# A hybrid decoder step on one core: the first head's projection made between the state space steps and read back from DRAM

## The chip, the cores and the metric

The kernel runs on one core of one Trainium2 chip. The metric is the device time of one execution in microseconds, the median of several executions. A core has TensorE (PE, with its weight loads as PEld), VectorE (DVE), ScalarE (ACT), GpSimd (POOL), SyncE (SP, which here issues most DMAs) and 16 DMA engines.

## What is computed

One layer of a hybrid decoder, for 1024 prompt tokens and 8 x 4 sample tokens (1056 rows), width 1024, in float32. One RMSNorm feeds one projection w_in, whose columns go to four attention heads (q, k, v, gate ga) and to a state space branch (u, gate gs). Both branches are gated, joined and go through w_out into the residual stream.

```python
xn = _rmsnorm(hp, norm_g[l])
q, k, v, ga, u, gs = _in_proj(xn, w_in[l], q_norm_g[l], k_norm_g[l])   # q, k normed per 64
o = _diff_attend(q, k, v, ...)           # softmax(q1 k1) - lam * softmax(q2 k2), times v
o_a = _attn_out(o, ga, subln_g[l], lam_init)              # norm, times silu(ga)
o_s, hr, hi = _s5_branch(u, gs, h0_re, h0_im, ...)        # scan; gelu; glu; times silu(gs)
hp = hp + jnp.concatenate([o_a, o_s], axis=-1) @ w_out[l]
```

Outputs are the new rows, the normed keys, the values and the last states, of prompt and samples.

## The kernel before, in words

A float32 product is made of three matmuls of rounded parts (high x high, high x low, low x high), all through the helper `mm` (L138). A weight block of 128 rows and 512 columns comes as a tile `wraw` (3 buffers) and is split into `ws` (9 buffers) by `split_w`: ScalarE rounds (L187), VectorE or GpSimd in turn subtracts (L190). The transposed input lies in SBUF as `xt` tiles, already split. PSUM has three buffers `acc` for projections, two each of `sc` and `tr`, one `pv`.

The program has three parts. **First phase** (`first_phase`, L330): the state space branch. The order of TensorE's work is written by hand in the table `UNITS` (L45); the other engines are ordered by the scheduler. A unit is a letter and a number: `C` a chunk of the u projection (24 matmuls 128x352, `u_part`), `G` a chunk of the gate projection (24 such matmuls, then two VectorE passes L411 and L413 around a ScalarE tanh L412, and a store on ScalarE's queue L414; 12 chunks in all, from the generator `gate`), `T` statistics of the rows, `D` their spread over columns (the `tr<-diag,ones` matmuls), `M` and `N` maps and kernels of a group of channels, `L`, `S`, `O` loading u, the states and the output of a group, `Z`, `H` reading z and the gates back, `Y` the glu (`acc<-z,ws`, 36 matmuls each), `A`, `B`, `Q`, `P`, `U`, `W`, `X` small ones. In the states VectorE and GpSimd run a long chain (`St`, `X`, `H`, L724 to L756) with TensorE before and after it.

**Heads** (`project`, L858, mixed by a model clock with `attention` and `sample_attend`, L232): for each of four heads and each pair j of token tiles, 2 x 24 matmuls with a 128-row tile of x as the stationary operand and 512 weight columns (q, k, v, ga of the head) moving. Then the aftercare: v is scaled into `vo`; `norm_qk` squares (ScalarE L846), reduces (VectorE L847), makes a reciprocal root by small operations (L850, L162 to L169) and multiplies (L854); `silu` (L902, L903) makes the gate. Some steps later `keep_qkv` (L905) transposes q and k (L913) and writes their rounded parts (L922 to L927) into a tile `pt`, 1536 wide, 6 buffers; the scores read it. The samples have 16 matmuls per head (`project_sample`, L932). After a head's last pair the weights of the next are loaded. Row tile t of the projection is in PSUM until its last reader is done.

**Output projection** (`finish`, `out_proj`, L1206 on).

```python
        w = self.load_w(self.w_in_head(0), KT)
        ...
        self.mix((self.project(w), 1.0), (self.attn, RATE1), (self.smp, RATE3), until=True)
```

## Time and profile before

| what | value |
|---|---|
| runs shown | 677.31 us median of 3 (675.5 to 678.51) |
| profiled execution | 677.01 us |
| its span, first to last instruction | 675.2 us |
| busy: TensorE matmuls, weight loads | 589.8 us (87%), 489.0 us (72%) |
| busy: VectorE, ScalarE, GpSimd | 488.6 us (72%), 296.5 us (44%), 160.2 us (24%) |
| mean granted TensorE clock | 0.959 |
| first 512-wide matmul of the heads | 231.2 us into the span |

The page of the profile gives busy time per engine, the span in 40 slices, the chain of waits that ended last and the costliest groups of instructions. The trace behind it answers closer: busy time by window, an engine's timeline with the idle time ahead of each piece and what ended it, groups of instructions with the mean duration of one, and DMA issues with the time to landing.

### The profile page before, as it was taken

Reading aid. Unit: us, or ns where it says so; the run is one execution under the profiler, and the core shown is the slowest. Engines: PE = TensorE matmul, PEld = TensorE weight load, DVE = VectorE, ACT = ScalarE, POOL = GpSimd, SP = SyncE. Lnnn points to the kernel's source line nnn. Section 1 sums busy time; section 2 is a strip of 40 time slices with the busy share of each in tenths; the row PEclk is TensorE's granted clock in tenths of the full one; section 3 lists DMA queues with packets and bytes.
Section 4 is the critical chain, followed back from the end, with each engine's and each line's share of the span. In section 5 each row is a group of like instructions: output and inputs, shape, how many; then the busy total and the mean of one; then the engine's idle time right before and its main releaser. Section 6 shows DMA issues by size and latency. Waiting matters only on the chain.

```text
span 675.2 us, 10961 instructions
## 1 busy us (share of the span) xinstructions
PE 589.8 (87%) x3490; PEld 489.0 (72%) x3490; DVE 488.6 (72%) x1536; ACT 296.5 (44%) x732; POOL 160.2 (24%) x165
## 2 busy tenths in 40 slices
PE   5928589559598999989999899998999988999997
PEld 4926488558487877768877678776787756886775
DVE  5978997999774446898668986689866898822111
ACT  6952232111363325565455654556545577411000
POOL 0682779677522400020000200002000020001100
PEclk9968789798988999999999999999999998999999
DMA  9755418242366440243012431124301257333221
GB/s 308 259 158 150 84 48 223 78 149 71 94 191 200 147 136 26 67 126 111 24 34 72 123 109 25 34 67 127 109 17 33 58 164 219 129 112 124 83 82 51
DMA packets 85735, 74.61 MB, mean 110 GB/s; under 512 B 8685, under 2 KB 74766, under 8 KB 85678
## 3 DMA queue, kind: packets, MB, share of 16 engines
q1 hardware_dynamic: 83374, 69.51, 34.3%
q10 hardware_dynamic: 2304, 4.41, 1.8%
q8 instruction: 28, 0.46, 0.3%
q14 instruction: 29, 0.24, 0.1%
HBM read 53.85 MB, written 20.04 MB: 109 GB/s over the span
## 4 chain that ended last, share of the span: by engine, by line
PE 43%; DVE 30%; DMA 9%; ACT 6%; POOL 6%; issue 5%; SPq 1%; POOLq 0%; DVEq 0%; ACTq 0%
PE acc L138 31%; PE sc L138 5%; PE pv L138 3%; DVE s L1036 3%; DMA xtok<-in_x 2%; PE tr L1061 2%; DVE ws L190 2%; DVE pt L927 2%; DVE pt L924 2%; DMA gz<-gsd 1%; POOL ws L190 1%; POOL gz L484 1%; DVE et L517 1%; DMA wraw<-in_w_out 1%; DVE s L164 1%
## 5 line engine op out<-in xcount | busy, mean ns | idle before, releaser
L138 PE MATMUL acc<-ws,xt 128*128 128x512 f32 x768 | 206.0, 405 | 0.4 <-DVE gz L508 0.4
L138 PEld LDWEIGHTS acc<-ws,xt 128*128 128x128 f32 x768 | 136.7, 189 | 26.4 <-issue 1.6
L190 POOL TENSOR_TENSOR ws<-wraw,ws 128x512 fp32r<-128x512 f32 x30 | 46.1, 1540 | 373.8 <-ACT ws L187 373.8
L138 PE MATMUL acc<-xt,ws 128*128 128x352 f32 x576 | 99.0, 332 | 8.4 <-ACT ws L187 7.8
L138 PEld LDWEIGHTS acc<-xt,ws 128*128 128x128 f32 x576 | 95.0, 193 | 11.2 <-ACT ws L187 8.1
L138 PE MATMUL acc<-ws,o 128*128 128x512 f32 x336 | 84.8, 400 | 4.5 <-ACT o L1222 1.8
L138 PEld LDWEIGHTS acc<-ws,o 128*128 128x128 f32 x336 | 62.9, 191 | 18.9 <-ACT o L1222 2.0
L1041 ACT ACTIVATE s<-s,mn 128x128 f32<-128x128 f32 (+7 forms) x64 | 49.4, 774 | 36.6 <-DVE mn L1036 36.2
L138 PE MATMUL sc<-pt 128*128 128x256 f32 (+1 forms) x320 | 57.6, 295 | 5.8 <-DVE pt L927 2.5
L138 PEld LDWEIGHTS sc<-pt 128*128 128x128 f32 x320 | 46.5, 189 | 22.2 <-DVE pt L927 5.9
L187 ACT ACTIVATE ws<-wraw 128x512 fp32r<-128x512 f32 x68 | 41.4, 626 | 38.2 <-PE acc L138 20.3
L1270 DVE TENSOR_TENSOR xres<-acc,xres 128x512 f32<-128x512 f32 x16 | 11.0, 690 | 51.9 <-PE acc L138 51.9
L138 PE MATMUL pv<-vo,wt 128*128 128x128 f32 x288 | 40.1, 279 | 0.0
L138 PEld LDWEIGHTS pv<-vo,wt 128*128 128x128 f32 x288 | 36.6, 191 | 3.5 <-ACT wt L1064 1.8
L190 DVE TENSOR_TENSOR ws<-wraw,ws 128x512 fp32r<-128x512 f32 x38 | 32.5, 858 | 7.0 <-ACT ws L187 7.0
L412 ACT ACTIVATE acc<-gs 128x352 f32<-128x352 f32 x12 | 5.6, 468 | 62.8 <-DVE gs L411 62.8
L138 PE MATMUL acc<-z,ws 128*128 128x352 f32 x144 | 25.8, 338 | 5.1 <-DVE gs L413 3.2
L138 PEld LDWEIGHTS acc<-z,ws 128*128 128x128 f32 x144 | 24.4, 198 | 6.4 <-DVE gs L413 3.5
L1061 PE MATMUL tr<-cn,s 128*128 128x128 f32 x144 | 26.0, 274 | 1.3 <-ACT wt L1064 0.8
L1036 DVE CUSTOM_DVE_ANT_0 s<-sc,cb 128x512 f32<-128x512 f32 (+3 forms) x48 | 26.3, 548 | 1.1 <-PE sc L138 0.7
L1046 DVE SCALAR_TENSOR_TENSOR s<-s,ls 128x128 f32<-128x128 f32 (+7 forms) x32 | 26.0, 812 | 0.4
L1064 ACT ACTIVATE wt<-tr 128x512 f32<-128x512 f32 (+3 forms) x48 | 22.9, 485 | 6.6 <-PE tr L1061 6.5
(289 smaller groups left out, 1028.9 us busy)
## 6 DMA issues: line engine op xcount, KB each, us to landing
wraw<-in_w_in SPq DMA_DIRECT2D x44, 256.0 KB, 3.1
xT<-in_xT SPq DMA_DIRECT2D x12, 352.0 KB, 7.2
xtok<-in_x SPq DMA_DIRECT2D x8, 512.0 KB, 5.1
cached<-in_cache_k SPq DMA_DIRECT2D x64, 64.0 KB, 1.9
cached<-in_cache_v SPq DMA_DIRECT2D x64, 64.0 KB, 1.9
...
```

The lines of the kernel that those rows point to most:

```text
L138: self.nc.tensor.matmul(out, lhsT, rhs, start=start, stop=stop)
L164: v.tensor_tensor(tmp, tmp, x, op=OP.mult)
L187: nc.scalar.activation(hi, raw, AF.Copy)
L190: (nc.vector if self.turn else nc.gpsimd).tensor_tensor(lo, raw, hi.bitcast(F32), op=OP.subtract)
L924: v.scalar_tensor_tensor(lo[ps], q[ps], self.gains[ps, 0:1], hi[ps].bitcast(F32), op0=OP.mult, op1=OP.subtract)
L927: v.scalar_tensor_tensor(kk[half[1]], k[ps], self.pkc("k_g")[ps], kk[half[0]].bitcast(F32), op0=OP.mult, op1=OP.subtract)
L1036: v.tensor_tensor_reduce(out=s[:, k0 + a0:k0 + a1], in0=q[:, a0:a1], in1=bias, op0=OP.add, op1=OP.min, scale=1.0, scalar=last, accum_out=m)
L1041: nc.scalar.activation(s[:, 0:L], s[:, 0:L], AF.Exp, bias=last, scale=-1.0, accum_out=ls[:, 2 * i + c:2 * i + c + 1])
L1046: v.scalar_tensor_tensor(wv, st[1][:, 0:L], cf, wv, op0=OP.mult, op1=OP.add)
L1061: nc.tensor.transpose(q[:, 128 * b:128 * b + 128], wv[:, 128 * (b0 + b):128 * (b0 + b) + 128], self.idn)
L1064: nc.scalar.activation(wt[:, 0:128 * bn], q[:, 0:128 * bn], AF.Copy)
L1270: v.tensor_tensor(x, a, x, op=OP.add)
```

## The change

Head 0's projection leaves the heads. Its eight weight blocks are loaded in two halves of 256 columns by a new unit `V` (`half_head`). A new unit `J` is one step of `first_head`: for one half and one of nine row tiles 24 matmuls 128x256 (16 for the sample tile, 64x256), a ScalarE copy into `ho` and a store on ScalarE's queue to `h_d` in DRAM; there are 18 of them, set between the other units. The table `UNITS` is written anew: the chunks C30 and C21 stand ahead of D0, and most gate chunks stand earlier. The projection then runs over heads 1 to 3. With each pair of head 1 comes a `stored_pair` of head 0: it reads 512 KB of `h_d` into `hx` (one buffer) and has the same aftercare as a projected pair. Queries and keys get tiles of their own, `qt` (1024 wide, 4 buffers) and `kt` (512 wide, 8 buffers); `vo` goes from 5 to 8 buffers, `ga` from 3 to 5; the program is built with a setting for a DMA scratch size.

```diff
-UNITS = ("M0 T0 C20 D0 U0 L0 W N0 M1 P0 C30 X U1 L1 C21 C32 S0 N1 C31 C22 U2 L2 O0 M2 G G U3 S1 G N2 L3 G O1 "
+UNITS = ("M0 T0 C20 C30 C21 D0 U0 L0 W N0 M1 P0 X U1 L1 C31 C22 C32 S0 N1 G U2 L2 G O0 M2 G G U3 S1 G G N2 L3 G V0 G G O1 M3 G P1 "
+         "G S2 J J N3 G V1 J J J S3 Q0 J J Z1 J A0 J J O2 Z0 J B0 Z2 J J O3 J H0 Z3 J J H1 J J H2 Y0 H3 Y1 Y2 Y3").split()
...
+VB = 8
+GB = 5
+HB = 1
...
-        w = self.load_w(self.w_in_head(0), KT)
+        w = self.load_w(self.w_in_head(1), KT)
...
+        hs, self.w0 = self.first_head(), []
...
+                elif c[0] == "V":
+                    self.turn = None
+                    self.w0.append([self.split_w(r) for r in self.half_head(int(c[1]))])
+                elif c[0] == "J":
+                    next(hs)
...
+    def half_head(self, half):
+
+        w = self.w_in_head(0)
+        for k2 in range(KT // 2):
+            raw = self.raws.tile([128, W], F32, name="wraw", tag="wraw", bufs=3)
+            r = raw.rearrange("p (k s c) -> p k s c", k=2, s=2)
+            for i in range(2):
+                self.nc.sync.dma_start(r[:, i], w(2 * k2 + i)[:, 2 * half:2 * half + 2])
+            yield raw
+
+    def first_head(self):
+
+        nc = self.nc
+        self.h_d = self.dr.tile([NTOK, W], F32, name="hd")
+        for half in range(2):
+            for t in range(9):
+                n = 128 if t < 8 else 32
+                a = self.acc()[:, 0:256]
+                for kt in range(KT):
+                    c = 256 * (kt % 2)
+                    wh, wl = (x[:, c:c + 256] for x in self.w0[half][kt // 2])
+                    if t < 8:
+                        xh, xl = (self.A[kt][:, z, 128 * t:128 * t + 128] for z in (0, 1))
+                        self.mm(a, xh, wh, kt == 0, False)
+                        self.mm(a, xh, wl, False, False)
+                        self.mm(a, xl, wh, False, kt == KT - 1)
...
+                o = self.ss.tile([128, 256], F32, name="ho", tag="ho", bufs=3)[0:n]
+                if t < 8:
+                    nc.scalar.activation(o, a, AF.Copy)
...
+                nc.scalar.dma_start(self.h_d[128 * t:128 * t + n, 256 * half:256 * half + 256], o)
+                yield
...
+    def stored_pair(self, j, st):
+
+        x = self.att.tile([128, 2, W], F32, name="hx", tag="hx", bufs=HB)
+        self.nc.sync.dma_start(x, self.h_d[256 * j:256 * j + 256, :].rearrange("(i p) c -> p i c", i=2))
+        vo = self.value(st, j)
+        for i in range(2):
+            self.nc.scalar.activation(vo[:, i, :], x[:, i, 256:384], AF.Copy, scale=self.xr[:, 2 * j + i:2 * j + i + 1])
+        self.pair(0, j, st, [x[:, 0], x[:, 1]])
...
-        for h in range(NH):
+        first = self.new_head()
+        for h in range(1, NH):
+            st = self.new_head()
             for j in range(4):
+                if h == 1:
+                    self.stored_pair(j, first)
+                    if j == 1:
+                        s = self.att.tile([32, W], F32, name="ssum", tag="ssum", bufs=1)
+                        nc.sync.dma_start(s, self.h_d[S:NTOK, :])
+                        self.sample_due(0, s, first)
...
-        pt = st["PT"][j] = self.pt("pt")
+        qt = st["Q"][j] = self.att.tile([128, 1024], F32R, name="qt", tag="qt", bufs=4)
+        kt = st["K"][j] = self.att.tile([128, 512], F32R, name="kt", tag="kt", bufs=8)
...
-    nc = bacc.Bacc("TRN2", target_bir_lowering=False, num_devices=1)
+    nc = bacc.Bacc("TRN2", target_bir_lowering=False, num_devices=1, dynamic_dma_scratch_size=1024)
```

Here `pair` holds what followed a pair's matmuls before (norm, gates, the due `keep_qkv`), and `value` hands out `vo`.

What this does to the order of the engines' work is shown at three places. The first is TensorE after the third group's states (`sc<-U,BT`, `tr<-U,BT`), ahead of the last group's map and kernel (`tr<-cn,W`, `tr<-G,bd`). Before:

```order
L138 MATMUL sc<-U,BT 64x145 x4
L138 MATMUL tr<-U,BT 64x145 x4
L138 MATMUL sc<-U,BT 64x145 x4
L138 MATMUL tr<-U,BT 64x145 x4
L690 MATMUL tr<-cn,W 128x128 x8
L138 MATMUL tr<-G,bd 32x128 x8
L138 MATMUL acc<-xt_84,ws 128x352 x3
```

Now the last rows of the second J (`acc<-ws,xt`, 256 wide) stand there:

```order
L141 MATMUL acc<-ws,xt_86 128x256 x3
L141 MATMUL acc<-ws,xt_87 128x256 x3
L141 MATMUL acc<-ws,xt_88 128x256 x3
L141 MATMUL acc<-ws,xt_89 128x256 x3
L141 MATMUL acc<-ws,xt_90 128x256 x3
L141 MATMUL acc<-ws,xt_91 128x256 x3
L737 MATMUL tr<-cn,W 128x128 x8
L141 MATMUL tr<-G,bd 32x128 x8
L141 MATMUL acc<-xt_84,ws 128x352 x3
```

Sixteen rows of three 256-wide matmuls, two J's, have come in between the states and the kernel.

The second place is TensorE in the first 512-wide matmuls of the heads, around the first transposes of a head's pair. Before, with 72 such matmuls ahead:

```order
L138 MATMUL acc<-ws,xt_89 128x512 x3
L138 MATMUL acc<-ws,xt_90 128x512 x3
L138 MATMUL acc<-ws,xt_91 128x512 x3
L913 MATMUL tr<-cn,qn 128x128 x4
L138 MATMUL acc<-ws,xt_84 128x512 x3
L138 MATMUL acc<-ws,xt_85 128x512 x3
L138 MATMUL acc<-ws,xt_86 128x512 x3
```

Now the transposes (L990) of head 0's first stored pair stand among the first 48 matmuls of head 1, and the first scores (`sc<-kt,qt`) too:

```order
L141 MATMUL acc<-ws,xt_85 128x512 x3
L141 MATMUL acc<-ws,xt_86 128x512 x3
L141 MATMUL acc<-ws,xt_87 128x512 x2
L990 MATMUL tr<-cn,qn 128x128
L141 MATMUL acc<-ws,xt_87 128x512
L990 MATMUL tr<-cn,qn 128x128 x3
L141 MATMUL acc<-ws,xt_88 128x512 x3
L141 MATMUL acc<-ws,xt_89 128x512 x3
L141 MATMUL acc<-ws,xt_90 128x512 x3
L141 MATMUL acc<-ws,xt_91 128x512 x2
L141 MATMUL sc<-kt,qt 128x128 x2
L141 MATMUL acc<-ws,xt_91 128x512
```

The transposes come after 35 wide matmuls of the heads, where they came after 72.

The third place is SP's queue at the same point (`gz<-gsd` reads gates, `osd<-gz` stores the branch, `TB` is the bias table). Before:

```order
L481 DMA gz<-gsd_1718 128x1056
L509 DMA osd<-gz 128x1056
L179 DMA wraw<-in_w_in 128x4x128
L977 DMA TB<-tbd 32x256 x2
L509 DMA osd<-gz 128x1056
L977 DMA TB<-tbd 32x256 x2
```

Now the first read of the stored head stands behind the weight load:

```order
L528 DMA gz<-gsd_1497 128x1056
L556 DMA osd<-gz 128x1056 x2
L182 DMA wraw<-in_w_in 128x4x128
L923 DMA hx<-hd 128x2x512
L556 DMA osd<-gz 128x1056
L1059 DMA TB<-tbd 32x256 x4
```

The stored pair's load is behind one weight load and ahead of the last store of the branch.

## Rows read from the trace of the kernel before

**Rows 1.** Part 1 of the page: busy us (share of the span) xinstructions.

```profile
PE 589.8 (87%) x3490; PEld 489.0 (72%) x3490; DVE 488.6 (72%) x1536; ACT 296.5 (44%) x732; POOL 160.2 (24%) x165
```

**Rows 2.** Part 4 of the page: the chain that ended last, by engine.

```profile
PE 43%; DVE 30%; DMA 9%; ACT 6%; POOL 6%; issue 5%; SPq 1%; POOLq 0%; DVEq 0%; ACTq 0%
```

**Rows 3.** Busy time by window: us, busy (x) of PE, PEld, DVE, ACT, POOL; PEclk, DMA share, GB/s.

```profile
38.00:134.00 96.00, 61.46 (x423) 56.31 (x424) 84.61 (x159) 27.42 (x60) 65.47 (x62) 0.82 0.43 116
134.00:155.00 21.00, 13.28 (x107) 11.68 (x105) 21.00 (x34) 5.75 (x13) 16.93 (x12) 0.86 0.45 136
155.00:231.00 76.00, 62.97 (x392) 59.29 (x392) 50.94 (x76) 28.87 (x51) 32.64 (x29) 0.93 0.45 142
231.00:305.50 74.50, 71.17 (x408) 55.00 (x409) 53.11 (x216) 36.12 (x99) 8.12 (x8) 1.00 0.33 94
305.50:560.70 255.20, 242.46 (x1484) 191.40 (x1483) 205.67 (x842) 143.92 (x388) 17.20 (x13) 1.00 0.26 76
560.70:676.00 115.30, 108.56 (x516) 86.61 (x514) 42.12 (x113) 23.96 (x56) 4.78 (x3) 0.99 0.33 109
```

**Rows 4.** TensorE's timeline, 38 to 231 us: start, us, work, [idle before <-releaser].

```profile
53.53 3.91 PE L138 MATMUL tr<-diag,ones 128*128 128x384 f32 x6 [15.78 <-DVE diag L314]
...
80.69 1.97 PE L690 MATMUL tr<-cn,W 128*128 128x128 f32 x8 [7.48 <-ACT St L724]
...
99.96 7.98 PE L138 MATMUL acc<-xt,ws 128*128 128x352 f32 x48
...
128.62 0.82 PE L138 MATMUL sc<-H,G 128*128 128x137 f32 x2 [7.31 <-DVE kk L700]
...
149.91 1.12 PE L690 MATMUL tr<-cn,W 128*128 128x128 f32 x4 [5.92 <-ACT St L724]
...
185.18 1.50 PE L138 MATMUL tr<-bias,rn 33*32 33x384 f32 x8 [7.13 <-ACT Z L775]
...
204.27 5.15 PE L138 MATMUL acc<-z,ws 128*128 128x352 f32 x22 [3.19 <-DVE gs L413]
```

**Rows 5.** TensorE's timeline after 231 us.

```profile
231.20 16.91 PE L138 MATMUL acc<-ws,xt 128*128 128x512 f32 x72 [0.39 <-DVE gz L508]
...
262.11 3.92 PE L138 MATMUL acc<-ws,xs 128*64 128x512 f32 x16
...
271.29 1.19 PE L138 MATMUL sc<-pt 128*128 128x256 f32 x8
272.32 1.32 PE L138 MATMUL acc<-ws,xt 128*128 128x512 f32 x5
```

**Rows 6.** Groups of VectorE, 231 to 600 us, forms apart: busy us, mean ns of one.

```profile
L190 DVE TENSOR_TENSOR ws<-wraw,ws 128x512 fp32r<-128x512 f32 x19 | 15.4, 810 | 3.0 <-ACT ws L187 3.0
...
L847 DVE TENSOR_REDUCE qss<-qn 128x4 f32<-128x256 f32 x32 | 13.1, 411 | 6.7 <-ACT qn L846 6.3
...
L163 DVE SCALAR_TENSOR_TENSOR qt<-qr 128x8 f32<-128x8 f32 x16 | 2.7, 168 | 0.5
...
L854 DVE TENSOR_TENSOR qn<-acc,qr 128x256 f32<-128x256 f32 x32 | 12.1, 418 | 0.6
...
L923 DVE CAST pt<-pt 64x256 fp32r<-64x256 f32 x32 | 9.2, 289 | 19.9 <-ACT pt L922 19.5
...
L924 DVE SCALAR_TENSOR_TENSOR pt<-tr,gains,pt 64x256 fp32r<-64x256 f32 x32 | 15.5, 483 | 0.8
```

**Rows 7.** ScalarE: a group of 231 to 600 us; a DMA issue in its timeline.

```profile
L846 ACT ACTIVATE qn<-acc 128x256 f32<-128x256 f32 x32 | 12.0, 374 | 0.0
...
183.57 0.33 ACTq L414 DMA_DIRECT2D gsd<-gs  x1
```

**Rows 8.** SP's timeline at 231 us; part 6 of the page: KB each, us to landing.

```profile
231.86 0.38 SPq L179 DMA_DIRECT2D wraw<-in_w_in  x1
...
xtok<-in_x SPq DMA_DIRECT2D x8, 512.0 KB, 5.1
```

**Rows 9.** VectorE's timeline: the last multiply of head 0's projection.

```profile
305.52 0.76 DVE L854 TENSOR_TENSOR qn<-acc,qr 128x256 f32<-128x256 f32 x2
```

More of the change, by code (lines that the diff above doesn't have):

```diff
@@ L416, in gate @@
                     self.gs_d[m] = d
-                yield
+                yield m
     def u_part(self, m, n):
@@ L856, in norm_qk, with new_head, pair, value @@
         return qn
+    def new_head(self):
+        st = {"ga": {}, "Q": {}, "K": {}, "V": {}, "kept": {}, "out": set()}
+        self.heads.append(st)
+        return st
+    def pair(self, h, j, st, accs):
+        qn = self.norm_qk(accs, 128, self.xe[:, 2 * j:2 * j + 2])
+        ga = st["ga"][j] = self.att.tile([128, 2, 128], F32, name="ga", tag="ga", bufs=GB)
+        for i in (0, 1):
+            self.silu(ga[:, i, :], accs[i][:, 384:512], self.xh[:, 2 * j + i:2 * j + i + 1])
+        vo = st["V"][j]
+        self.due.append((self.clock + DUE, lambda: self.keep_qkv(h, j, qn, vo, st)))
+    def value(self, st, j):
+        st["V"][j] = self.att.tile([128, 2, 128], F32, name="vo", tag="vo", bufs=VB)
+        return st["V"][j]
+    def stored_pair(self, j, st):
[5 more added lines that the diff above has]
+        self.pair(0, j, st, [x[:, 0], x[:, 1]])
+    def sample_due(self, h, s, st):
+        qn = self.sample_columns(h, s, st)
+        self.due.append((self.clock + DUE, lambda: self.keep_sample(h, qn, st)))
     def project(self, w):
@@ L919, in keep_qkv @@
             for c, ps in enumerate(half):
-                hi, lo, kk = (pt[:, 512 * z + 256 * c:512 * z + 256 * c + 256] for z in range(3))
+                hi, lo = (qt[:, 512 * z + 256 * c:512 * z + 256 * c + 256] for z in range(2))
+                kk = kt[:, 256 * c:256 * c + 256]
                 ot = half[1 - c]
@@ L1232, in out_proj @@
             yield None
-        PT, out = (self.heads[NH - 1][n] for n in ("PT", "out"))
+        Q, out = (self.heads[NH - 1][n] for n in ("Q", "out"))
         c0 = 0
```

42 lines of the change are left out of this document (20 added, 22 removed).

## The prediction

> **What bounds the kernel now.** I read the page's busy shares first. TensorE's matmuls are busy in 87% of the span, VectorE in 72% [rows 1], and the chain that ended last runs over TensorE for 43% and VectorE for 30% [rows 2]: neither alone sets the time. So the next view is busy time by stage [rows 3]. From 231 us to the end TensorE is the bound: 71.2 of 74.5 us, 242.5 of 255.2, 108.6 of 115.3. Before that it is not: in the three windows from 38 to 231 us it is busy for 61.5 + 13.3 + 63.0 = 137.7 of 193 us, 55.3 us idle, and VectorE for 156.6; from 134 to 155 us VectorE is busy all the time. TensorE's timeline [rows 4] names the idle stretches, in brackets with what ended each: 15.78 us before the spread step, then 7.48, 7.31, 5.92, 7.13 and 3.19 us, all ended by VectorE or ScalarE in the chain of the state space steps; these are 46.8, and pieces of under 3 us make up the other 8.5. So there is idle TensorE time in one stage and a full TensorE in the next.
>
> **What the change removes.** Head 0's projection goes out of the heads: 4 pairs of 48 matmuls 512 wide and 16 for the samples. A long run of them takes 16.91 / 72 = 0.235 us each, the 16 take 3.92 [rows 5]: 192 x 0.235 + 3.92 = 49.0 us, in a stage where TensorE has some 5% idle. If nothing else held it, the heads would be 49 us shorter.
>
> **What it adds between the state space steps.** The 18 steps J issue 16 x 24 = 384 matmuls 256 wide over all tiles and 2 x 16 narrow ones. A run of eight 256-wide ones starts at 271.29 and the next group at 272.32: 0.129 us each [rows 5]. The widths 352 (7.98 / 48 = 0.166) and 512 (0.235) extrapolate to 0.125, so I take 0.129: 416 x 0.129 = **53.7 us**. Bounds: half of a 512-wide one, 0.118, gives 49; the 0.166 of a 352-wide one gives 69, and I stay near the low end because the eight were measured at this width.
>
> **What of it lies in the gaps.** I go by the new order, gap by gap. The two u chunks moved ahead of the spread step (48 matmuls, 8.0 us) fill half of the 15.78. The gate chunks moved ahead of the second output step (4.0 us each) fill the 7.31 and 0.9 beside it. Two J's (3.1 each) ahead of the last kernel map fill 6.2 of the 5.92 and what is around it. The J's around the last two output steps and the glu steps fill 7.13, 3.19 and small ones, 12.2 in all. That is 34.6 us; the 7.48 stays. The stage grows by 53.7 - 34.6 = 19.1. A denser stage also wins back a little clock: the granted clock is 0.82, 0.86 and 0.93 in these windows [rows 3], and 22 matmuls after the 3.19 us wait took 5.15 us, 0.234 each where 0.166 is usual [rows 4]. I take 2 us, so **+17.1**. Bounds: 53.7 less 47 (all but the 7.48) is +7; with 20 filled it is +34, because every gate chunk needs two VectorE passes before its PSUM buffer is free (three buffers), and VectorE is full from 134 to 155.
>
> Small things of this stage. Eight weight splits of head 0 come earlier, four of them on VectorE at 0.81 us [rows 6]: 3.2 us against 36 us of VectorE idle in 38 to 231; without that cover, 3.2. Each J adds one ScalarE copy (a 128x256 one from PSUM takes 0.374 [rows 7]) and one issue on ScalarE's queue (0.33 in the timeline [rows 7]), 18 x 0.7 = 12.7 us, while ScalarE is busy for 62 of 193 us [rows 3]. The 16 half loads on SP's queue are 16 issues of 0.38 [rows 8]. I cost these at nothing. So with the wider rings, the two tiles for queries and keys (the same instructions), and the scratch setting: no rows change by it that I can see; if some buffer is short, that is inside the upper bound.
>
> **What the stored head costs in the heads.** The projection goes, its aftercare stays: per pair two reductions 0.411, nine small operations of about 0.166, two multiplies 0.418, four casts 0.289, two gate products about as long, four subtractions 0.48 [rows 6], 6.8 us of VectorE per pair, and about 2.9 for the samples: 4 x 6.8 + 2.9 = 30.1 us. Before, head 0's stretch, from 231 to the last multiply of its projection at 305.52 [rows 9], held one head's aftercare: 53.1 us of VectorE in 74.5 [rows 3]. Now the stretch of the first projected head (head 1) holds two, and more of head 0's attention: counting both orders row by row with these durations, VectorE gets 42 us more up to the last multiply of head 1, 30 of aftercare and 12 of attention. That is 53.1 + 42 = **95 us of VectorE**, against TensorE's 79 (the same 208 wide matmuls, 74.5, and 4 of scores). So this stretch changes its bound. It starts late too: the first stored pair needs 512 KB from DRAM, which SP issues behind the first weight load of the next head; that load is issued 0.7 us into the stage [rows 8], a 512 KB load lands 5.1 us after issue [rows 8], so about 6 us. Head 0's transposes stand behind 35 matmuls (8.2 us) in TensorE's order, with the pair's aftercare ahead of them, so TensorE waits there. Between the 1.00 that VectorE shows from 134 to 155 us and the 0.806 (205.7 / 255.2) of the steady heads, I take 0.97, nearer the first because little but VectorE would hold this stretch: 95 / 0.97 + 6 = 104 us, 25 more than TensorE's 79. The later stretches keep TensorE as bound. **Heads: -49 + 25 = -24.** Bounds: no late start and VectorE without any gap, 95 us, gives -49 + 16 = -33; occupancy 0.806 gives 95 / 0.806 + 6 = 124, so -49 + 45 = -4.
>
> The stored pairs share one buffer: the load of the second waits on SP's queue until VectorE is done with the first, and holds up what stands behind it there (weights of head 2, cache pages, stores of values). With some 25 us from pair to pair and a landing of 5.1, I cost that at nothing; were it not hidden, it is 5.1 us for each of three pairs, part of rival 2's price.
>
> **The sum.** 677.0 (profiled execution; 675.2 of span and 1.8 around it; the median of the runs shown is 677.3, 0.3 above) + 17.1 - 24 = 670.1, say **670 us**.
>
> **Weighed against a rule.** In the steady heads VectorE is busy for 205.7 and weight loads for 191.4 of 255.2 us, matmuls for 242.5 [rows 3]. The Trainium skill, "Perfetto Trace Analysis", section Identifying the Most-Contended Engine, says that matmul busy time is no good measure of TensorE and that one should set its weight-load share beside the occupancy of the other engines. By that, VectorE (81%) and not TensorE (75%) would be the engine to relieve, and matmuls taken away there would buy little: the second rival below, 690 us for 670. The trace speaks for TensorE in one respect: its idle time there is 12.7 us of 255.2, and the waits in it are short.
>
> **Rivals.**
> 1. *The gaps take nearly all of it and VectorE packs without gaps.* For it: 55.3 us idle against 53.7 of work. Against: the 7.48 and the first 15.78 lie where head 0's weights are not loaded yet. Growth 7 - 2 = 5, heads -33: 677 + 5 - 33 = 649.
> 2. *Slower: the first heads are paced by VectorE at its steady occupancy.* Place: the stretch of head 1. VectorE's operations there stand in chains with ScalarE (squares, tanh, copies) between them, so that it may not exceed the 0.806 seen. Price: 124 us for 79, gain 4 against a growth of 17.1: 677 + 17.1 - 4 = 690. It decides below an occupancy of 95 / 105 = 0.90, where the stretch takes 111 us and the gain equals the growth. For it: no stretch of the heads shows more than 0.81. Against: there TensorE was the bound.
> 3. *The gaps are not filled.* The gate chunks and J's wait for PSUM buffers that VectorE frees late, and shift the state space chain with them: 20 us filled, growth 34 - 2 = 32: 677 + 32 - 24 = 685.
> 4. *It does not do what it says.* The new order does show head 0's matmuls ahead of the last glu step and none behind it, so hardly: 677.
>
> **How the numbers follow.** My forecast (658 to 681 by itself) gets 0.46, rival 1 0.20, rival 2 0.17, rival 3 0.15, rival 4 0.02. A measurement of this kernel tells 0.5%, 3.4 us, from no change. Faster: 0.30 of the forecast and 0.20 of rival 1, 0.50. Within 0.5%: 0.11 + 0.03 + 0.03 + 0.02 = 0.19. Slower: 0.05 + 0.14 + 0.12 = 0.31. The range reaches from rival 1 to just beyond rival 2, 648 to 691; about one in ten lies beyond each end.
>
> **What would show it.** The first 512-wide matmul of the heads starts at about 231.2 + 17 = 248 us; later than 258 is rival 3, before 240 rival 1. In TensorE's timeline J's stand where the 5.92, 7.13 and 3.19 us waits were. From the first 512-wide matmul to the last multiply of head 1 it takes about 104 us, with VectorE over 95% busy and TensorE waiting for VectorE, the first wait being for the stored pair; 115 us or more with VectorE at 85% is rival 2. From there to the end the time is about the same as TensorE's work: no new waits. The prediction is wrong if the heads are shorter by under 10 us or over 40 us, or if the stage before them grows by more than 30.

## The result and the profile after

| | before | after |
|---|---|---|
| median of 7 runs each | 676.93 us (673.66 to 678.51) | 680.63 us (678.00 to 683.19) |
| ratio, 95% interval | | 1.0056 [1.0032, 1.0079] |
| profiled execution, its span | 677.01, 675.2 us | 678.00, 676.2 us |
| first 512-wide matmul of the heads | 231.20 us | 265.71 us |
| from there to the end of the span | 444.0 us | 410.5 us |

The change is slower by 0.56%; I had forecast 670 us. The profiled execution of after happens to be the lowest of its seven, so that the two spans differ by 1.0 us where the medians differ by 3.7. What happened is seen in either: the stage ahead of the heads grew by 34.5 us and the heads, up to the end, shrank by 33.5. The page, its parts 1 and 4, answers to [rows 1, 2]:

```profile
PE 596.3 (88%) x3698; PEld 502.8 (74%) x3698; DVE 467.8 (69%) x1537; ACT 304.8 (45%) x750; POOL 155.0 (23%) x165
PE 41%; DVE 29%; DMA 11%; POOL 6%; issue 6%; ACT 5%; POOLq 0%; SPq 0%; ACTq 0%; DVEq 0%
```

On the page nothing stands out: TensorE has 208 instructions and 6.5 us more (the narrower matmuls), VectorE 21 us less, and the chain still alternates between the two. The stages have to be looked at. Busy time by window of after, columns as in [rows 3]; the cuts are the third group's states (the first `sc<-U,BT` of that group), the heads' first 512-wide matmul, the last multiply of head 1's projection and the output projection:

```profile
38.00:161.69 123.69, 91.83 (x597) 85.91 (x595) 104.38 (x203) 35.27 (x73) 75.83 (x74) 0.86 0.44 123
161.69:265.71 104.02, 95.34 (x746) 92.42 (x745) 46.39 (x73) 40.60 (x77) 40.40 (x35) 0.97 0.46 136
265.71:374.60 108.89, 96.18 (x579) 70.24 (x580) 88.66 (x378) 62.56 (x167) 8.34 (x8) 0.97 0.42 121
374.60:557.20 182.60, 170.28 (x1068) 134.02 (x1067) 149.87 (x650) 108.63 (x300) 11.53 (x9) 0.99 0.25 73
557.20:676.20 119.00, 113.49 (x554) 91.78 (x553) 48.59 (x139) 28.01 (x67) 4.77 (x3) 0.99 0.32 105
```

The same view of before, cut at the same two places of the first stage, at 141.79 and 231.20 us:

```profile
38.00:141.79 103.79, 69.25 (x470) 63.89 (x471) 92.40 (x169) 28.23 (x62) 72.75 (x69) 0.84 0.46 125
141.79:231.20 89.41, 68.46 (x449) 63.39 (x448) 64.35 (x101) 34.02 (x62) 42.49 (x33) 0.90 0.42 131
```

Read these two against the first two of after. Up to the third states, TensorE's idle time was 103.8 - 69.3 = 34.5 us and is now 123.7 - 91.8 = 31.9: hardly anything was filled. The states came 19.9 us later, about as much as the five gate chunks take that were moved ahead of this point (24 x 0.166 = 4.0 us each). Behind it the idle time went from 21.0 to 8.7 us, so there the J's did fill 12.3, and the granted clock rose from 0.90 to 0.97. In all TensorE's idle time of the stage went from 55.5 to 40.5: 15.0 us filled.

TensorE's timeline of after, 38 to 280 us, answers to [rows 4]; the waits of 3 us and more, the third states, and the start of the heads:

```profile
54.56 2.90 PE L141 MATMUL tr<-diag,ones 128*128 128x384 f32 x4 [8.03 <-DVE diag L317]
...
83.53 1.11 PE L141 MATMUL tr<-G,bd 128*32 128x128 f32 x16 [6.08 <-POOL G L721]
...
102.83 0.83 PE L141 MATMUL sc<-H,G 128*128 128x137 f32 x2 [7.98 <-POOL H L798]
...
135.83 1.10 PE L141 MATMUL tr<-G,bd 128*32 128x128 f32 x16 [8.96 <-ACT BT L738]
...
161.69 0.71 PE L141 MATMUL sc<-U,BT 128*64 128x145 f32 x8
...
210.47 0.85 PE L141 MATMUL tr<-bias,rn 33*32 33x384 f32 x8 [3.01 <-ACT Z L822]
...
265.71 8.35 PE L141 MATMUL acc<-ws,xt 128*128 128x512 f32 x35
...
275.87 0.30 PE L990 MATMUL tr<-cn,qn 128*128 128x128 f32 x1 [1.82 <-DVE qn L898]
```

The first line is as planned: 15.78 before the spread step became 8.03. The 7.31 before the second output, the 5.92 before the last map and the 3.19 are gone, and the 7.13 is 3.01; in the glu steps waits of 2.47 and 2.13 us are left. But two waits stand here that [rows 4] does not have: 7.98 us at the first output (`sc<-H,G` at 102.83) and 8.96 us at the third group's kernel (`tr<-G,bd` at 135.83). In before, the same two places waited 2.71 and 1.39 us:

```profile
94.92 0.82 PE L138 MATMUL sc<-H,G 128*128 128x137 f32 x2 [2.71 <-POOL H L751]
...
116.37 0.67 PE L138 MATMUL tr<-G,bd 128*32 128x128 f32 x16 [1.39 <-POOL G L674]
```

So 7.98 - 2.71 + 8.96 - 1.39 = 12.8 us of what was filled ahead of the third states were given back.

**Where the 8.96 comes from.** The kernel's transposes need `BT`, which ScalarE copies out of PSUM. ScalarE's timeline of after, just ahead:

```profile
128.89 0.47 ACT L459 ACTIVATE acc<-gs 128x352 f32<-128x352 f32 x1 [10.02 <-DVE gs L458]
...
132.75 0.63 ACT L190 ACTIVATE ws<-wraw 128x512 fp32r<-128x512 f32 x1 [2.84 <-DVE gs L460]
134.70 0.47 ACT L459 ACTIVATE acc<-gs 128x352 f32<-128x352 f32 x1 [1.33 <-DVE gs L458]
135.10 1.07 ACT L738 ACTIVATE BT<-tr 128x512 f32<-128x512 f32 x2
```

The copy stands behind two tanh of gate chunks (L459) in ScalarE's order. The first of these waits 10.02 us for a gate's VectorE pass L458. Between the two, ScalarE issues that gate's store at 132.30, and this waits 2.84 us more for the gate's second pass, L460. VectorE makes both passes only after a group's scan. Its timeline, the end of that chain:

```profile
127.17 0.66 DVE L791 TENSOR_TENSOR X<-E_re,X 128x512 f32<-128x512 f32 x1
...
128.35 0.51 DVE L458 SCALAR_TENSOR_TENSOR gs<-acc,R 128x352 f32<-128x352 f32 x1
```

In before the copy stood ahead of such a tanh, so that only the tanh waited:

```profile
114.58 1.08 ACT L691 ACTIVATE BT<-tr 128x512 f32<-128x512 f32 x2 [0.53 <-PE tr L690]
...
124.70 0.47 ACT L412 ACTIVATE acc<-gs 128x352 f32<-128x352 f32 x1 [8.52 <-DVE gs L411]
```

**Where the 7.98 comes from.** The first output waits for the first group's scan chain on VectorE and GpSimd. That chain begins with a multiply into `X`. VectorE's timeline of before has it at 82.49 us:

```profile
82.49 0.68 DVE L730 TENSOR_TENSOR X<-E_re,St 128x512 f32<-128x512 f32 x1
```

That of after has it at 90.55, behind a weight split and a multiply of u:

```profile
80.94 3.09 DVE L193 TENSOR_TENSOR ws<-wraw,ws 128x512 fp32r<-128x512 f32 x1
...
88.49 2.13 DVE L490 TENSOR_TENSOR uT<-uT,R 128x1024 f32<-128x1024 f32 x1
90.55 0.67 DVE L777 TENSOR_TENSOR X<-E_re,St 128x512 f32<-128x512 f32 x1
```

Both stand there because TensorE now makes the u chunks earlier: the multiply is of a u chunk, and the split is of a gate's weights, whose buffer is free only when the u chunks are done with it. They make 5.2 of the 8.1 us; what made the rest was not followed up.

### The profile page after: what moved, and what is told of

It is laid out like the page before. It is cut to its first block, busy times and chain, and to the rows that moved or that the text cites. A ratio compares the mean times of both kernels' runs of the same rounds, so it can differ in the third digit from the quotient of the medians.

```text
span 676.2 us, 11416 instructions
## 1 busy us (share of the span) xinstructions
PE 596.3 (88%) x3698; PEld 502.8 (74%) x3698; DVE 467.8 (69%) x1537; ACT 304.8 (45%) x750; POOL 155.0 (23%) x165
## 4 chain that ended last, share of the span: by engine, by line
PE 41%; DVE 29%; DMA 11%; POOL 6%; issue 6%; ACT 5%; POOLq 0%; SPq 0%; ACTq 0%; DVEq 0%
PE acc L141 26%; PE sc L141 6%; PE pv L141 4%; DVE s L1117 3%; PE tr L1142 2%; DVE ws L193 2%; DMA ud<-uT 2%; DMA wraw<-in_w_in 1%; DMA hx<-hd 1%; PE tr L141 1%; POOL X L778 1%; DMA C<-in_c 1%; DVE qt L1002 1%; DMA osd<-gz 1%; DVE s L1127 1%
## 5 line engine op out<-in xcount | busy, mean ns | idle before, releaser
L141 PE MATMUL acc<-ws,xt 128*128 128x512 f32 (+1 forms) x960 | 209.8, 360 | 0.4 <-DVE gs L460 0.2
L141 PEld LDWEIGHTS acc<-ws,xt 128*128 128x128 f32 x960 | 149.2, 192 | 21.1 <-issue 3.3
L193 POOL TENSOR_TENSOR ws<-wraw,ws 128x512 fp32r<-128x512 f32 x30 | 40.4, 1352 | 344.9 <-ACT ws L190 267.7
L141 PE MATMUL acc<-xt,ws 128*128 128x352 f32 x576 | 101.1, 338 | 8.8 <-ACT ws L190 8.8
L141 PEld LDWEIGHTS acc<-xt,ws 128*128 128x128 f32 x576 | 98.0, 199 | 11.1 <-ACT ws L190 8.8
L141 PE MATMUL sc<-kt,qt 128*128 128x256 f32 (+1 forms) x320 | 57.7, 295 | 11.2 <-DVE mn L1117 4.3
L141 PEld LDWEIGHTS sc<-kt,qt 128*128 128x128 f32 x320 | 46.1, 190 | 25.9 <-DVE mn L1117 8.2
L1122 ACT ACTIVATE s<-s,mn 128x128 f32<-128x128 f32 (+7 forms) x64 | 49.5, 774 | 29.8 <-DVE mn L1117 23.5
L193 DVE TENSOR_TENSOR ws<-wraw,ws 128x512 fp32r<-128x512 f32 x38 | 30.4, 804 | 27.1 <-ACT ws L190 26.9
L1351 DVE TENSOR_TENSOR xres<-acc,xres 128x512 f32<-128x512 f32 x16 | 11.0, 689 | 53.2 <-PE acc L141 53.2
L1117 DVE CUSTOM_DVE_ANT_0 s<-sc,TB,mn 128x256 f32<-128x256 f32 (+1 forms) x56 | 24.7, 442 | 0.8
```

The lines of the kernel that those rows point to most:

```text
L141: self.nc.tensor.matmul(out, lhsT, rhs, start=start, stop=stop)
L193: (nc.vector if self.turn else nc.gpsimd).tensor_tensor(lo, raw, hi.bitcast(F32), op=OP.subtract)
L1117: v.tensor_tensor_reduce(out=s[:, k0 + a0:k0 + a1], in0=q[:, a0:a1], in1=bias, op0=OP.add, op1=OP.min, scale=1.0, scalar=last, accum_out=m)
L1122: nc.scalar.activation(s[:, 0:L], s[:, 0:L], AF.Exp, bias=last, scale=-1.0, accum_out=ls[:, 2 * i + c:2 * i + c + 1])
L1351: v.tensor_tensor(x, a, x, op=OP.add)
```

## The experiments

The theories. **A:** the places cost the time. TensorE's new order changed which instructions of ScalarE and VectorE stand ahead of the state space chain, and two moved places, the gate chunks ahead of the last two maps and the two u chunks ahead of the spread, make the chain late. **B:** 53 us of projection don't fit in this stage, wherever they are put. **C**, a form of B: any TensorE work put in the gaps delays the chain. A pair of numbers in what follows is the heads' first 512-wide matmul (before 231.20, after 265.71) and the ratio to before. The heads' start is that of one profiled execution each: two of the same kernel (e7 and e12) differ in it by 1.1 us, and e9, whose first stage is that of after, by 5.1 from after. So two or three microseconds of it are no evidence without a wait that explains them. Diffs of `UNITS` show the piece that differs.

**e1_map_before_chunks.** The change, with the third map ahead of two gate chunks.

```diff
...
-U3 S1 G G N2 L3 G V0
+U3 S1 N2 G G L3 G V0
...
```

> Theory A (queues): gate chunks and u chunks that were moved ahead put their VectorE passes, ScalarE tanhs and weight splits into queues in front of the state space chain, so idle TensorE time is moved and not filled. Rival theory B (TensorE): the stage grew because the steps J do not fit; moving the chunks cost nothing. Here the kernel map of the third group (N2) stands ahead of the two gate chunks instead of behind them. A: the 8.96 us wait for the copy of BT falls under 2 us, because that copy no longer stands behind two tanhs on ScalarE; the heads start at 257 to 259 us instead of 265.7, time 672 to 675 us. B: what follows is bound by the work of TensorE, the start stays at 264 to 267, time 679 to 682.

Measured: 677.90 us, 1.0016 [0.9992, 1.0039]; heads at 263.02, both between what A and what B expected. TensorE's timeline:

```profile
118.81 0.66 PE L738 MATMUL tr<-cn,W 128*128 128x128 f32 x4 [0.23 <-ACT St L772]
...
135.46 0.96 PE L142 MATMUL acc<-xt,ws 128*128 128x352 f32 x2 [3.62 <-DVE gs L461]
```

The 8.96 is gone, so its cause was the place. The heads start only 2.7 us earlier: the gate chunks, now behind the map, wait there for a gate's second VectorE pass (L461) that frees a PSUM buffer, the 3.62. A holds for the wait and was too large for the time.

**e4_u_chunks_back.** The change, with the u chunks where before has them, and with the first two gate chunks together ahead of the first output.

```diff
...
-C20 C30 C21 D0 U0 L0 W N0 M1 P0 X U1 L1 C31 C22 C32 S0 N1 G U2 L2 G O0
+C20 D0 U0 L0 W N0 M1 P0 C30 X U1 L1 C21 C32 S0 N1 C31 C22 U2 L2 G G O0
...
```

> The changed kernel with the u chunks where they were before (C30 and C21 not ahead of the spread step; gate chunks behind the first group's states). A: weight splits and u multiplications no longer stand ahead of the first group's states on VectorE, the chain starts at 83 to 85 us instead of 90.5, and the 7.98 us wait for H falls to 2 to 4: time 673 to 677. B: the gap of 15.8 us ahead of the spread step opens again and 8 us of TensorE work come back behind it: 681 to 689.

Measured: 678.33 us, 1.0019 [0.9988, 1.0049]; heads at 264.05.

```profile
54.48 4.08 PE L142 MATMUL tr<-diag,ones 128*128 128x384 f32 x6 [15.88 <-DVE diag L318]
80.62 1.97 PE L738 MATMUL tr<-cn,W 128*128 128x128 f32 x8 [6.27 <-ACT St L772]
...
132.53 1.11 PE L142 MATMUL tr<-G,bd 128*32 128x128 f32 x16 [9.90 <-ACT BT L739]
```

The 7.98 at the first output is gone and the 15.88 before the spread is back: filling the first gap had only moved it (8.03 + 6.08 + 7.98 = 22.1 us of waits up to the first output in after, 15.88 + 6.27 = 22.2 here). The wait falls as A expected, and further; the time lies above A's range and below B's. The intervals of e1 and e4 each overlap that of the change, so neither gain is shown by itself.

**e7_both_back and e12_both_back_again.** Both edits together, and the same kernel once more in five rounds.

> The edits of e1 and e4 together (third kernel map ahead of the gate chunks; u chunks where they were). A, if the two losses are separate: the heads start at 258 to 261 us, 673 to 676 us. If a wait that is taken away here turns up at the next buffer instead: start at 262 to 265, 677 to 680.

> The kernel of e7 once more, in more rounds, to tell it from the kernel before. If its gain over the changed kernel is real it stands at 672 to 676 us, 0.2 to 0.8% under the kernel before; if e7 was a lucky draw, at 677 to 680.

Measured: 674.54 us, 0.9985 [0.9939, 1.0032], heads at 260.58; and 675.93 us, 0.9993 [0.9975, 1.0011], heads at 261.68. The two places together are worth 4 to 5 us of the stage and turn the change from slower into no difference; the interval of the second, longer measurement lies wholly below the change's. The heads still start 30 us later than in before. So A's two places explain the change's loss, but not why the stage grows.

**e2_order_alone.** Before, with after's order of u and gate chunks and no projection in it (no V, no J).

```diff
...
-UNITS = ("M0 T0 C20 D0 U0 L0 W N0 M1 P0 C30 X U1 L1 C21 C32 S0 N1 C31 C22 U2 L2 O0 M2 G G U3 S1 G N2 L3 G O1 "
-         "M3 G P1 G S2 N3 Q0 G G S3 Z1 G A0 G O2 Z0 B0 Z2 O3 H0 Z3 H1 G H2 G Y0 H3 Y1 Y2 Y3").split()
+UNITS = ("M0 T0 C20 C30 C21 D0 U0 L0 W N0 M1 P0 X U1 L1 C31 C22 C32 S0 N1 G U2 L2 G O0 M2 G G U3 S1 G G N2 L3 G G G O1 "
+         "M3 G P1 G S2 N3 G S3 Q0 Z1 A0 O2 Z0 B0 Z2 O3 H0 Z3 H1 H2 Y0 H3 Y1 Y2 Y3").split()
...
```

> The kernel before with the new order of the u and gate chunks and without V and J: head 0 stays in the heads. A: the second output step starts near 150 us as in the changed kernel (129 before), and with five chunks fewer behind it the heads start at 236 to 243 us (231 before): 682 to 688 us. B: the order is neutral, heads start at 231, 675 to 679 us.

Measured: 689.07 us, 1.0178 [1.0130, 1.0225]; heads at 243.22, just beyond A's range, so 12.0 us are lost with the same work.

```profile
101.18 0.82 PE L138 MATMUL sc<-H,G 128*128 128x137 f32 x2 [8.08 <-POOL H L751]
...
134.17 1.11 PE L138 MATMUL tr<-G,bd 128*32 128x128 f32 x16 [9.16 <-ACT BT L691]
...
182.32 0.82 PE L138 MATMUL sc<-U,MT 128*128 128x137 f32 x2 [5.97 <-ACT St L724]
195.97 0.82 PE L138 MATMUL sc<-H,G 128*128 128x137 f32 x2 [6.62 <-POOL H L751]
220.29 0.66 PE L138 MATMUL acc<-z,ws 128*128 128x352 f32 x1 [8.41 <-ACT z L1290]
```

The two new waits come without the projection, so the order makes them. The last three are gaps that the gate chunks had covered; with the chunks gone forward they open, and in after the J's had to fill these first.

**e15_better_order_alone.** As e2, with the order of e7 instead.

```diff
...
-C20 C30 C21 D0 U0 L0 W N0 M1 P0 X U1 L1 C31 C22 C32 S0 N1 G U2 L2 G O0 M2 G G U3 S1 G G N2
+C20 D0 U0 L0 W N0 M1 P0 C30 X U1 L1 C21 C32 S0 N1 C31 C22 U2 L2 G G O0 M2 G G U3 S1 N2 G G
...
```

> The kernel before with the order of e7 and without V and J (as e2, with e7's order). e2 started its heads 12.0 us later than before. A sharper: the waits at the first output and the third map made most of that, so the start is at 233 to 238 us: 679 to 684. If five gate chunks ahead of the second output cost by themselves, it stays at 241 to 245: 687 to 691.

Measured: 685.48 us, 1.0121 [1.0095, 1.0146]; heads at 241.58, 10.4 us later than in before: the start is in the second branch's range, the time between the two. By the heads' start the two places are 1.6 of e2's 12.0 us, by the ratios some 4; the larger part comes with the moving of the five gate chunks itself (the one other unit that moves with them is Q0, the load of the glu's weights). TensorE's timeline:

```profile
154.66 0.71 PE L138 MATMUL sc<-U,BT 128*64 128x145 f32 x8
...
180.56 0.83 PE L138 MATMUL sc<-U,MT 128*128 128x137 f32 x2 [6.04 <-ACT St L724]
194.21 0.82 PE L138 MATMUL sc<-H,G 128*128 128x137 f32 x2 [6.70 <-POOL H L751]
218.80 0.66 PE L138 MATMUL acc<-z,ws 128*128 128x352 f32 x1 [7.40 <-ACT z L1290]
```

The third states come 12.9 us later than in before, for 19.9 in after: of the chunks' 20 us some 7 are now hidden. The gaps that the chunks had covered behind the states are open as in e2: from the states to the heads it takes 241.58 - 154.66 = 86.9 us, for 231.20 - 141.79 = 89.4 in before, though 20 us of chunks have left this part. So 17.5 of the 20 us had lain in gaps there. My sharper expectation of A fell here.

**e5_idle_matmuls.** Before, plus five units K of 24 matmuls 128x352 that nobody reads (5 x 4.0 = 20 us), about where after has its added gate chunks: gate chunks without VectorE or ScalarE work.

```diff
...
-S0 N1 C31 C22 U2 L2 O0 M2 G G U3 S1 G N2 L3 G O1
+S0 K N1 C31 C22 U2 L2 K O0 M2 G G U3 S1 G K N2 L3 G K K O1
...
+                elif c[0] == "K":
+                    a = self.acc()
+                    for kt in range(KT):
+                        for z in range(3):
+                            self.mm(a[:, 0:352], self.A[kt][:, 0, 128 * z:128 * z + 128], self.A[kt][:, 0, 0:352], kt == 0 and z == 0, kt == KT - 1 and z == 2)
...
```

> The kernel before, order and all, with five added chunks of 24 matmuls 128x352 whose results nobody reads (20 us of TensorE, nothing on any other engine): one ahead of the second kernel map, one ahead of the first output, one ahead of the third kernel map, two ahead of the second output, about where the change put its moved gate chunks. A: work of TensorE alone does fill the idle time there (7.48, 2.71, 1.39 and 7.31 us), so the heads start at 233 to 238 us (231.2 before): 679 to 684 us. Rival C (any work on TensorE in these places delays the chain, whatever its passes): start at 247 to 252, 693 to 698 us.

Measured: 684.20 us, 1.0104 [1.0077, 1.0131]; heads at 239.49, 8.3 us later, 1.5 us beyond A's range and far from C's. ScalarE's timeline has the `BT` copy behind a tanh, and the wait for that gate's second pass, here too, with no pass added anywhere:

```profile
126.92 0.47 ACT L417 ACTIVATE acc<-gs 128x352 f32<-128x352 f32 x1 [8.81 <-DVE gs L416]
...
130.69 1.09 ACT L696 ACTIVATE BT<-tr 128x512 f32<-128x512 f32 x2 [3.30 <-DVE gs L418]
```

So it is not VectorE's added work that did it. TensorE reaching the map one chunk later was enough for the scheduler to put the copy behind the tanh.

**e14_idle_matmuls_after_map.** As e5, with the third K behind the map.

```diff
...
-S1 G K N2 L3
+S1 G N2 K L3
...
```

> The kernel of e5 with the one idle chunk that stood ahead of the third kernel map behind it; the same 20 us of added TensorE work. In e5 that map's copy on ScalarE came to stand behind a tanh that waits for VectorE, and TensorE waited 9.7 us, as in the changed kernel, though no pass was added. If the place in ScalarE's queue and not the work is what costs (A in its sharper form), the wait goes, and the heads start at 230 to 234 us instead of 239.5: 676 to 680. If added TensorE work as such delays the chain (C), the start stays at 238 to 241: 682 to 686.

Measured: 679.45 us, 1.0049 [1.0027, 1.0071]; heads at 235.56, 4.4 us later than in before for the same 20 us, between the two branches and nearer to A's.

```profile
118.33 0.67 PE L138 MATMUL tr<-G,bd 128*32 128x128 f32 x16 [1.69 <-ACT BT L696]
```

One unit's place was worth 3.9 us of the stage, and 15.6 of 20 us of bare TensorE work are hidden. C falls as a general rule: this stage has room for matmuls. Up to the third states these 20 us cost 6.7 (148.47 for 141.79). The same 20 us as gate chunks, with their VectorE and ScalarE passes and at partly other places, cost 12.9 there in e15 and 19.9 in after.

**e3_third_of_j.** After, with only the first of the three products for the prompt rows in J; the two products with a low part are left out of head 0's projection.

```diff
...
-                        self.mm(a, xh, wh, kt == 0, False)
-                        self.mm(a, xh, wl, False, False)
-                        self.mm(a, xl, wh, False, kt == KT - 1)
+                        self.mm(a, xh, wh, kt == 0, kt == KT - 1)
...
```

> The steps J make one of their three products for the prompt rows (the two with low parts are left out): 256 of 384 matmuls, about 31 us of TensorE, go away; all else stays. A: the J's stand mostly in gaps and cost the stage about 13 us net, so 9 to 15 us are saved: 665 to 672. B: the J's are the growth of 34 us, so 25 to 33 us are saved: 648 to 656.

Measured: 665.23 us, 0.9814 [0.9765, 0.9863]; heads at 250.61. Taking away 256 matmuls (16 x 16, at the 0.128 us each that after shows for them, below: 33 us) brings the heads 15.1 us forward. So about half of what was taken away had lain in gaps, as A expected, and about half had been paid for. With two thirds of J gone the heads still start 19.4 us late, of which e2 gives 12.0 to the order alone.

**e8_steps_early.** After, with before's order of u and gate chunks, and the J's put in the early gaps instead, where the gate chunks were; it needs 12 buffers of split weights instead of 9, and `vo` and `ga` one less each.

```diff
...
-UNITS = ("M0 T0 C20 C30 C21 D0 U0 L0 W N0 M1 P0 X U1 L1 C31 C22 C32 S0 N1 G U2 L2 G O0 M2 G G U3 S1 G G N2 L3 G V0 G G O1 M3 G P1 "
-         "G S2 J J N3 G V1 J J J S3 Q0 J J Z1 J A0 J J O2 Z0 J B0 Z2 J J O3 J H0 Z3 J J H1 J J H2 Y0 H3 Y1 Y2 Y3").split()
+UNITS = ("M0 T0 C20 D0 U0 L0 W N0 M1 P0 C30 X U1 L1 C21 C32 S0 N1 C31 C22 V0 U2 L2 J O0 M2 G J G U3 S1 J G N2 L3 J G J "
+         "O1 M3 G J P1 G S2 V1 J J N3 J G G S3 Z1 G Q0 J A0 G J O2 Z0 J B0 Z2 J O3 H0 J Z3 G J H1 G H2 J J J Y0 H3 Y1 Y2 "
+         "Y3").split()
...
-VB = 8
-GB = 5
+VB = 7
+GB = 4
...
-        ws = (self.fp if more else self.wp).tile([128, 2, W], F32R, name="ws", tag="ws", bufs=NMORE if more else 9)
+        ws = (self.fp if more else self.wp).tile([128, 2, W], F32R, name="ws", tag="ws", bufs=NMORE if more else 12)
...
```

> The u and gate chunks in the order of before, and the steps J, which put no pass on VectorE, into the early gaps: one ahead of the first output, three ahead of the second, the rest as the change has them. For that three more ws buffers (12), with vo 7 and ga 4. A: the early idle time is filled by J's, the heads start at 250 to 257 us: 662 to 671. Rival C: the start stays at 264 or later, 677 to 684.

Measured: 699.56 us, 1.0336 [1.0306, 1.0366]; heads at 278.18. The time is in neither theory's range. TensorE's timeline:

```profile
103.62 2.71 PE L142 MATMUL acc<-ws,xt 128*128 128x256 f32 x11 [9.08 <-DVE ws L194]
```

The first J waits 9.08 us for a weight split that VectorE makes late, and holds up TensorE's order behind it. That is one cause of the 12.5 us more than in after; the others were not followed up.

**e10_one_u_chunk and e11_u_chunk_at_wait.** e7 with one u chunk ahead of the spread (e10), and also the next one ahead of the second map (e11).

```diff
...
-C20 D0 U0 L0 W N0 M1 P0 C30 X U1 L1 C21 C32 S0 N1 C31 C22
+C20 C30 D0 U0 L0 W N0 M1 P0 X U1 L1 C21 C32 S0 N1 C31 C22
...
```

And e11 against e10:

```diff
...
-C32 S0 N1 C31 C22 U2
+C32 S0 C31 N1 C22 U2
...
```

> The kernel of e7 with one u chunk (C30) ahead of the spread step and the other (C21) where it was. In e7 the copies of the first group's states on ScalarE stand behind the zero fill of C30's tile, which waits 10.3 us for GpSimd. A: with C30 earlier that wait goes, the 7.45 us wait ahead of the second kernel map falls under 3 us and the first output is no later than in e7 (about 96 us); the heads start at 255 to 259 us, 669 to 673. If the weight splits that C30 lets loose stand ahead of the state chain on VectorE, as in the changed kernel, the first output comes at 100 or later and the start stays at 260 to 263: 674 to 678.

> The kernel of e10 with the u chunk C31 ahead of the second kernel map instead of behind it; a u chunk has only a ScalarE copy behind it. A: it fills what is left of the wait there, start 1 to 3 us earlier than in e10: 667 to 672. If its copy on ScalarE stands ahead of the states' copies, the chain is later by as much and nothing is gained: as e10 or up to 3 us more.

Measured: 690.93 us, 1.0202 [1.0179, 1.0225], heads at 276.78; and 686.91 us, 1.0134 [1.0103, 1.0165], heads at 273.87. No branch expected that. TensorE's and VectorE's timelines of e10:

```profile
92.43 1.94 PE L738 MATMUL tr<-cn,W 128*128 128x128 f32 x8 [19.82 <-DVE W L563]
```

```profile
76.78 0.68 DVE L778 TENSOR_TENSOR X<-E_re,St 128x512 f32<-128x512 f32 x1
...
91.60 0.68 DVE L563 TENSOR_TENSOR W<-W,Wt 128x512 f32<-128x512 f32 x1
```

The first scan chain starts at 76.78, 5.7 us earlier than in before, and the product `W` that the second map needs now stands behind the whole chain on VectorE. TensorE waits 19.82 us. In e11 the same wait is 18.07. One chunk of 4 us, moved, costs 276.78 - 260.58 = 16.2 us of the stage.

**e9_casts_on_gpsimd and e13_two_hx** ask about the heads. e9 is after, with head 0's query casts on GpSimd instead of VectorE; e13 is e7 with two buffers for the stored pair, each pair loaded one ahead.

```diff
...
-                v.tensor_copy(hi[ot], hi[ps].bitcast(F32))
+                (g if h == 0 else v).tensor_copy(hi[ot], hi[ps].bitcast(F32))
...
-                v.tensor_copy(lo[ot], lo[ps].bitcast(F32))
+                (g if h == 0 else v).tensor_copy(lo[ot], lo[ps].bitcast(F32))
...
```

> The changed kernel with the 16 casts of head 0's queries on GpSimd instead of VectorE (16 x 0.289 = 4.6 us off VectorE in the first stretch of the heads). If VectorE paces that stretch by its amount of work, it gets 4 to 6 us shorter: 675 to 677. If it is paced by TensorE or by chains over several engines: no change, 679 to 682, or longer if GpSimd's casts are slower than VectorE's.

```diff
-HB = 1
+HB = 2
...
+        self.hx = []
+        self.load_stored(0)
...
-    def stored_pair(self, j, st):
-
+    def load_stored(self, j):
...
+        self.hx.append(x)
+
+    def stored_pair(self, j, st):
+
+        x = self.hx.pop(0)
+        if j < 3:
+            self.load_stored(j + 1)
...
```

> The kernel of e7 with two buffers for the stored pairs, each pair's load issued one pair ahead. If part of the first stretch of the heads (109 us, 12.7 us of it without TensorE) is waiting for these loads, the waits of head 0's transposes (6.1 us in the changed kernel) fall under 3 us and the time is 2 to 4 us under e7. If VectorE's chain of the aftercare is what they wait for, the load is already hidden and the time is that of e7 within 1 us.

Measured: e9 681.74 us, 1.0084 [1.0056, 1.0112]. Its window of the first stretch of the heads:

```profile
270.83:379.00 108.17, 95.72 (x576) 69.59 (x575) 85.09 (x355) 62.90 (x167) 15.34 (x24) 0.97 0.42 119
```

VectorE has 3.6 us less to do than in after, and the stretch is 0.7 shorter: the amount of VectorE's work doesn't pace it by itself. (A cast takes 0.41 us on GpSimd here and 0.30 on VectorE in after, so the chain through the casts did not get shorter; which of the two made the result is not told apart.) (The stage ahead, which the edit doesn't touch, took 5 us longer in this execution, the longest of e9's four; the heads to the end are 683.0 - 270.83 = 412.2 us, for 410.5.) e13: 675.07 us, 0.9975 [0.9954, 0.9996], the best version that does all the work: heads at 262.33, 408.6 us to the end for 410.4 in e7. The waits of head 0's transposes fall from 6.1 to 4.5 us, not under 3, and the time is 0.9 us under the same kernel with one buffer (e12), in the second branch's range. It is 0.25% faster than before, only just clear of no difference, and, by the two ratios, 0.8% faster than the change.

## Why the prediction was wrong

**The step that failed is "What of it lies in the gaps".** The sum was 53.7 of new work, less 34.6 in gaps, less 2 of clock. J's two groups among TensorE's instructions of after, 161.7 to 265.7 us, columns as in [rows 6]:

```profile
L141 PE MATMUL acc<-ws,xt 128*128 128x256 f32 x384 | 49.2, 289 | 0.3 <-DVE gs L460 0.2
...
L141 PE MATMUL acc<-ws,xs 128*64 128x256 f32 x32 | 4.0, 277 | 0.0
```

- *The added work:* 49.2 + 4.0 = 53.2 us, 0.128 each (the mean of one, 289 ns, counts the overlap of one with the next); forecast 53.7. TensorE's busy time from 38 us to the heads rose by 187.2 - 137.7 = 49.5, so the other matmuls took 3.7 us less, with the granted clock at 0.86 and 0.97 for 0.84 and 0.90; forecast 2.
- *The gaps:* 15.0 us were filled, not 34.6, and 49.5 - 15.0 = 34.5 is the growth; forecast 17.1, with a bound of 34. The moved chunks are the term that failed. Their 8.0 + 8.2 us were to lie in gaps, so the new order alone should have made the stage 16.2 us shorter; e2, which is that order alone, made it 12.0 longer. The J's put on it cost the other 22.5 (265.71 - 243.22), so 30.7 of their 53.2 us are hidden, more than the 18.4 that I had for them, as they also stand in gaps that the moved chunks left open. I filled gap by gap as though a gap stayed where it was. The chunks moved ahead of the spread moved that gap to the first output (7.98, undone by e4). The gate chunks moved ahead of the second output and the third map filled nothing net: the states behind them came later by about their 20 us, in part through a copy put behind a tanh (8.96, undone by e1), and the places they came from opened again (e2, e15: 12.0 and 10.4 us with no projection at all). That their passes on VectorE did the rest is not shown. Behind the third states the idle time fell by 12.3 us.
- *What I costed at nothing.* I set the J's copies and issues on ScalarE, 12.7 us, against its 62 busy of 193 us and costed them at nothing. No run shows that they cost more. But a share of busy time says nothing of the order in which an engine works: a copy that was there before, `BT` of 1.07 us, cost TensorE 8.96 us by its place, and of such places the sum had no term.

**The heads went the way I said, by more.** They shrank by 33.5 us; forecast 24, with a bound of 33. The stretch to the last multiply of head 1 took 108.9 us for the 104 forecast. VectorE was busy for 88.7, not 95, at 0.81 and not 0.97, which is rival 2's occupancy; but the stretch held more of TensorE's work than I had counted, 96.2 us for 79, as attention ran in it that would else come later (scores, `pv` and transposes) and the first matmuls of head 2. So the stretch holds 108.9 - 96.2 = 12.7 us of TensorE's idle time and not 25, and from its end to the end of the span it takes 301.6 us, where the forecast leaves 420 - 104 = 316. The late start cost TensorE little: its first wait for the stored pair is the 1.82 us at 275.87. The largest part is in one group of TensorE's instructions in this window, the transposes of a pair:

```profile
L990 PE MATMUL tr<-cn,qn 128*128 128x128 f32 x28 | 5.9, 303 | 6.1 <-DVE qn L898 6.1
```

Half of the idle time is theirs, for the last multiply `qn` of the aftercare on VectorE, as forecast. TensorE's busy time from the heads on, the last three windows of [rows 3] and of after, fell by 422.2 - 380.0 = 42.2 us, not 49. So TensorE was busy some 7 us longer with the matmuls that were left; about 3 us of it lie between 310 and 330 us:

```profile
290.00:310.00 20.00, 16.82 (x108) 11.86 (x106) 17.11 (x81) 12.43 (x37) 0.00 (x0) 1.00 0.36 97
310.00:330.00 20.00, 16.72 (x82) 12.09 (x83) 16.37 (x70) 10.24 (x25) 0.00 (x0) 0.83 0.24 76
```

The granted clock falls there to 0.83 in the mean, after 20 us with 3.2 idle; from 312 to 316 us it is 0.50, its lower level of 1.2 GHz. By the mean that is 16.72 x 0.17 = 2.8 us, an estimate; the other 4 were not followed up.

In the prediction I weighed the trace against the Trainium skill, "Perfetto Trace Analysis", section Identifying the Most-Contended Engine, which has TensorE's headroom judged by its weight-load share. I read from it that matmuls taken from the heads would buy little. It came out for the trace: 42.2 us of TensorE's busy time less bought 33.5.

**Rivals.** Rival 3, gaps not filled, has the size of what happened, growth 34.5 for its 32, and its sign "later than 258 us" was met, as was my own sign of being wrong, a stage that grows by more than 30. Its 685 was too high by the heads' better gain. Its mechanism is only half there: it stood on PSUM buffers that VectorE frees late, and in after TensorE's waits for these are 0.23, 2.47 and 2.13 us, all behind the third states, while the growth began ahead of them. What shifted the chain was the order of the other engines' instructions, which the change does not write down and yet moves, and which I had not put a price on. Rival 1 had the heads right and the stage wrong. Rival 2's mechanism shows in the occupancy and its price was wrong. That 680.63 us is only some 10 us from my 670 is in part luck: the heads' gain, 9.5 us better than forecast, hid more than half of an error of 17.4 us in the stage. What was left of the error was still enough to turn a forecast gain into a loss.

**What stays open.** What paces the first stretch of the heads: neither VectorE's amount (e9) nor the stored pair's load (e13, 1.8 us) does by much. The wider rings, the split tiles for queries and keys and the DMA scratch setting were not tried by themselves; e2 and e15 are without them, so they can have a part only in the 22.5 us of the J's and in the heads. And how far the stage could be filled, which is B's question: e14 hides 15.6 of 20 us of bare matmuls; the J's cost 260.58 - 241.58 = 19.0 us in e7 beyond e15, the same order without them, so some 34 of their 53.2 us are hidden there; and no run shows a version that keeps all the covered gaps covered.
